# Both parts of the normalised input as one moving operand of 512 columns, in a hybrid MLA and RWKV-7 encoder block

## The chip, the cores and the metric

One core of one Trainium2 chip runs the whole block. The time is that of one execution in device microseconds; before the change the median of 3 runs was 874.93 us (874.09 to 885.55).

## What is computed

One encoder layer on 256 positions of width 2048, batch 1, all in float32. The reference, cut to its products:

```
h    = rms_norm(x, g_pre)                       # 256 x 2048
proj = h @ w_in                                 # 2048 x 10688: q_a, kv_a, k_rope | r, k, v, low-rank parts | z_mla, z_rwkv | gates
q, kv = rms_norm(q_a) @ wq_b, rms_norm(kv_a) @ wkv_b
y_mla  = softmax attention, 8 heads of 128 + 64 rotary, 256 keys
y_rwkv = bidirectional RWKV-7 recurrence, 16 heads of 64, with a group norm and a bonus
merged = sigmoid(gate_mla) * ((y_mla * silu(z_mla)) @ w_br_mla) + sigmoid(gate_rwkv) * ((y_rwkv * silu(z_rwkv)) @ w_br_rwkv)
x + rms_norm(merged @ w_out, g_post)
```

## The kernel before, in words

**Two parts.** Every large product is done in float32r, in two parts: a tensor v is hi (v rounded by a copy) and lo = v - hi, and a product is hi hi + hi lo + lo hi, three TensorE passes. The weights are split on the way. A chunk of up to 128 x 1024 weights is loaded into one of 3 *raw* buffers by the SP queue; ScalarE copies it to *whi* (L327), VectorE subtracts into *wlo* (L330), with 3 buffers of each.

**Transposed products.** A projection task (`in_task`, through `cm_task`) makes 256 output channels x 256 positions: two halves of 128 channels, 16 steps of 128 rows of the weights (k), and for each the three passes at L396 to L398. The weights are stationary (128 x 128), h is the moving operand of 256 columns: *hhi* and *hlo*, each 128 x 16 x 256. Both halves of a task fill one PSUM bank (128 x 512). There are 32 such tasks besides the 8 of the second gate (`gate_rwkv_task`): 12 for r, k and v (`rwkv_tasks`), 8 of the first gate (`gate_mla_task`), 8 for z (`z_task`), 4 low-rank ones of attention (`low_rank_task`). A first product of the low-rank parts (L1531 onwards, four tiles of 96, 96, 128 and 128 channels) opens the kernel. The branch products (`um_task`, `ur_task`) have the same three passes over 8 steps; the output projection (`out_task`, L1334 to L1336) has the activations stationary and weights of 512 columns moving.

**The end of a task** reads its bank. r, k and v go through `mix` (two scaled ScalarE copies out of PSUM at L422, a VectorE addition, two VectorE operations); z through a tanh and one VectorE operation; the gates through a tanh; the low-rank ones through one copy (L549).

**Banks.** Of 8 PSUM banks, 3 (`DB`, in the trace d) serve the tasks and 5 (`MB`, m) the recurrence, the group sums, the transposes and attention; the key-value tasks move one from `MB` to `DB`, and the output projection takes all.

**The recurrence.** Four quads of 4 heads each. A quad is prepared (decay, keys, values), then `chunks_of` forms the masked products (L797), inverts triangular blocks of 32 x 32 on VectorE and goes through 4 steps: short passes (L912 to L944), between which one ScalarE and one VectorE copy bring 64 x 256 out of PSUM. A group norm follows. A quad's products wait for the quad before.

**The order.** The instructions of all engines are put in order by a planner at build time (`Streams`). Each part is a stream (a generator) that asks for an engine with a cost; the planner keeps the time at which each engine is free, adds a lag to each hand-over, and takes the request that can start first, by rank. `Free` holds lists of buffers or banks: `take` waits until one is in the list, `give` puts it back. A stream runs ahead of the time it asks for, so a buffer is back in the list as soon as its giver has been planned. The projection (`mm_stream`) has the lowest rank and fills TensorE. All engines then work through their lists in this order.

The sequence of tasks: the low-rank parts, r, k and v of the first quad, first gate, z and low-rank tasks mixed with the next quads' r, k and v, then `GPRE` second-gate tasks, 4 key-value tasks (they wait for the last quad), 4 query tasks with `MIX` second-gate tasks between, the 8 attention-branch tasks, the 8 recurrent-branch tasks, 4 output tasks. The tanh of a second-gate task is kept in a place that has come free: in the recurrence's buffers *u8* or *uv*, or in one of the general buffers (`W`) where more than `KEEP2` are free.

Of the kernel before, what the change touches and what calls it, by code (L numbers as in the profile page):

```python
# [15 lines left out]
S = 256  # L16
D = 2048
# [11 lines left out]
GPRE, MIX = 4, [0, 1, 1, 1]  # L29
# [9 lines left out]
KEEP, KEEP2 = 6, 9  # L39
# [4 lines left out]
class Streams:  # L44
# [6 lines left out]
    def __init__(self):  # L51
        self.free = dict.fromkeys("PADGS", 0.0)
        self.live = []
        self.used = dict.fromkeys("PADGS", 0.0)
        self.table = None
        self.mode = "128x128"

    def add(self, gen, rank, t=0.0):
        s = [gen, rank, t, None]
# [18 lines left out]
    def run(self, until=None):  # L78
        while self.live and not (until and until()):
            moved = True  # L80
            while moved:
                moved = False
                for s in list(self.live):
                    while s in self.live and s[3][0] in "WT" and (s[3][0] == "T" or s[3][1]()):
                        if s[3][0] == "T":
                            s[2] = max(s[2], s[3][1])
                        self._next(s, s[2])
                        moved = True
            if until and until():
# [19 lines left out]
            e, cost = s[3][0], s[3][1]  # L109
            if e == "P":  # L110
# [13 lines left out]
class Free:  # L124


    def __init__(self, tiles):
        self.tiles = list(tiles)
# [26 lines left out]
def encoder_block_kernel(  # L155
# [52 lines left out]
    hhi, hlo = sb([128, KT, S], "hhi", dt=F32R), sb([128, KT, S], "hlo", dt=F32R)  # L208
# [4 lines left out]
    W = Free(works[:-1])  # L213
    MB = Free(pps.tile([128, 512], F32, tag=f"m{i}", bufs=1, name=f"m{i}") for i in range(5))
    DB = Free(pps.tile([128, 512], F32, tag=f"d{i}", bufs=1, name=f"d{i}") for i in range(3))
# [7 lines left out]
    QP = Free(qpads)  # L223
# [15 lines left out]

    O = Streams()  # L240
# [130 lines left out]
    def cm_task(src, nk, xhi, xlo, mt, wd, end, kc=4, load_fn=None, ready=None, kready=None, k_first=0,  # L371
                begin=None, pairs=None, first_alone=False):

        parts = []
        nb = (len(mt) + 1) // 2
# [3 lines left out]
        for i, k0 in enumerate(k0s):  # L379
# [23 lines left out]
        def take():  # L403
            b = []
            for _ in range(nb):
                b.append((yield from DB.take()))
            return b

        add_task(parts, begin or take, end, ready)
# [56 lines left out]
    def ev_second(b):  # L466
        yield ("W", lambda: len(have.get("part", ())) == 2)
        for p, m, t, B in zip(b, (96, 128), have["part"], (DB, MB)):
            yield ("D", cD(512))
            tt(w2d(t)[0:m], w2d(t)[0:m], p2(p)[0:m], ALU.add)  # L470
            B.give(p)
# [48 lines left out]
    def ev_z(b, o):  # L520

        z = p2(b[0])
# [15 lines left out]
    def gate_mla_task(g):  # L538
        def end(b):
            yield ("A", cA(512), None, "exp")  # L540
            act.activation(m16[:, 2 * g:2 * g + 2], p2(b[0]), AF.Tanh, scale=0.5)
            DB.give(*b)
        in_task(GM0 + 256 * g, end)

    def low_rank_task(c0, key):
        def end(b):
            t = yield from W.take(KEEP)
            yield ("A", cA(512))
            act.copy(w2d(t), p2(b[0]))  # L549
            DB.give(*b)  # L550
# [492 lines left out]
    def wkv_task(g):  # L1043
        wkv_v = wkv_b.rearrange("(k p) c -> p k c", p=128)

        def begin():
            if g == 0:
                yield ("W", lambda: quads[3].done and len(MB.tiles) > 1)
                DB.give(MB.tiles.pop())
# [12 lines left out]
            a = yield from DB.take()  # L1062
# [591 lines left out]
```

## Time and profile before

| | |
|---|---|
| runs | 874.93 us median (874.09 to 885.55) |
| the profiled execution | 872.72 us, its span 870.9 us |
| TensorE busy, passes | 848.3 us (97%), 8112 |
| TensorE weight loads busy | 810.0 us (93%) |
| VectorE busy | 659.3 us (76%) |
| ScalarE busy | 501.1 us (58%) |
| granted TensorE clock | 0.998 |

In the rows, PE is TensorE, PEld its weight loads, DVE VectorE, ACT ScalarE, SP the queue that issues the loads. A name such as d<-hhi,whi is output <- moving operand, stationary operand; L396 is line 396 of the kernel before. Passes are pipelined: a pass's record lasts about 0.28 us although the next begins 0.12 us after it, so short waits do not show as idle time.

### The profile page before, as it was taken

The numbers are of one execution on the slowest core, as the hardware profiler recorded it, in microseconds if no ns is written. First come the engines' busy times: TensorE is split into PE (matmuls) and PEld (weight loads), VectorE is DVE, ScalarE is ACT, GpSimd is POOL, SyncE is SP. The second block draws the span as 40 slices with busy tenths as digits, with TensorE's granted clock in tenths as the row PEclk, the third lists the DMA queues.
The fourth block names the chain that finished last, engine by engine and source line by source line (L and its number), as shares of the span: only waits on it lengthen the run. The fifth ranks groups of instructions, "written<-read, shape, count | busy, mean of one in ns | idle before, by whom it ended". The sixth has DMA issues, their size and how long they took to land.

```text
span 870.9 us, 19398 instructions
## 1 busy us (share of the span) xinstructions
PE 848.3 (97%) x8112; PEld 810.0 (93%) x8112; DVE 659.3 (76%) x1082; ACT 501.1 (58%) x797; POOL 30.7 (4%) x66
## 2 busy tenths in 40 slices
PE   9999999999999999999999999999999999999996
PEld 8999999988899998999889999899999999998884
DVE  5878898868987878988789878775867556775554
ACT  6777644487544578354776445586766434444442
POOL 4110000000000000000000000000000000000000
PEclk9999999999999999999999999999999999999999
DMA  9565646633376523565423665346444675555553
GB/s 286 169 181 148 176 129 187 169 99 90 101 212 177 161 68 97 158 193 169 132 76 96 195 188 152 98 149 186 136 128 147 232 257 190 176 193 193 194 195 119
DMA packets 123528, 139.41 MB, mean 160 GB/s; under 512 B 6704, under 2 KB 110512, under 8 KB 123056
## 3 DMA queue, kind: packets, MB, share of 16 engines
q1 hardware_dynamic: 121664, 135.16, 52.4%
q0 software_dynamic: 768, 1.57, 0.6%
q10 hardware_dynamic: 1008, 1.44, 0.5%
q8 instruction: 63, 1.03, 0.5%
q14 instruction: 25, 0.20, 0.1%
HBM read 136.05 MB, written 2.10 MB: 159 GB/s over the span
## 4 chain that ended last, share of the span: by engine, by line
PE 73%; DVE 14%; ACT 8%; issue 2%; DMA 2%; DVEq 0%; ACTq 0%
PE d L396 16%; PE d L398 16%; PE d L397 15%; DVE wlo L330 4%; PE m L1334 2%; PE m L1335 2%; PE m L1336 2%; ACT whi L327 2%; DVE work L191 2%; PE m L398 2%; PE m L396 2%; PE m L397 2%; PE d L1335 1%; PE d L1334 1%; PE d L1336 1%
## 5 line engine op out<-in xcount | busy, mean ns | idle before, releaser
L327 ACT CAST whi<-raw 128x1024 fp32r<-128x1024 f32 (+3 forms) x252 | 252.8, 1004 | 254.2 <-PE d L397 155.1
L330 DVE TENSOR_TENSOR wlo<-raw,whi 128x1024 fp32r<-128x1024 f32 (+3 forms) x250 | 292.4, 1171 | 125.0 <-ACT whi L327 123.4
L396 PE MATMUL d<-hhi,whi 128*128 128x256 f32 (+1 forms) x1296 | 375.1, 289 | 0.0
L398 PE MATMUL d<-hhi,wlo 128*128 128x256 f32 (+1 forms) x1296 | 366.5, 283 | 2.3 <-DVE wlo L330 2.3
L397 PE MATMUL d<-hlo,whi 128*128 128x256 f32 (+1 forms) x1296 | 366.2, 283 | 0.0
L396 PEld LDWEIGHTS d<-hhi,whi 128*128 128x128 f32 (+1 forms) x1296 | 246.8, 190 | 4.5
L398 PEld LDWEIGHTS d<-hhi,wlo 128*128 128x128 f32 (+1 forms) x1296 | 246.9, 190 | 2.7 <-DVE wlo L330 2.7
L397 PEld LDWEIGHTS d<-hlo,whi 128*128 128x128 f32 (+1 forms) x1296 | 247.1, 191 | 0.1
L191 DVE TENSOR_TENSOR work<-work,work 128x512 f32<-128x512 f32 (+5 forms) x64 | 38.8, 612 | 3.9 <-ACT work L575 1.2
L191 DVE TENSOR_TENSOR u<-u,tmp 128x30 f32<-128x30 f32 (+7 forms) x120 | 29.9, 250 | 3.0
L191 DVE TENSOR_TENSOR tmp<-u 128x30 f32<-128x30 f32 (+7 forms) x120 | 29.8, 249 | 2.9
L396 PE MATMUL d<-b,whi 128*128 128x256 f32 x96 | 27.1, 282 | 0.0
L398 PE MATMUL d<-b,wlo 128*128 128x256 f32 x96 | 27.1, 282 | 0.0
L398 PE MATMUL d<-ar,wlo 128*128 128x256 f32 x96 | 27.0, 281 | 0.0
L397 PE MATMUL d<-work,whi 128*128 128x256 f32 x96 | 26.9, 280 | 0.0
L397 PE MATMUL d<-ar,whi 128*128 128x256 f32 x96 | 26.9, 280 | 0.0
L396 PE MATMUL d<-ar,whi 128*128 128x256 f32 x96 | 26.8, 279 | 0.0
L1334 PE MATMUL m<-whi,hhi 128*128 128x512 f32 x60 | 23.3, 389 | 0.0
L1335 PE MATMUL m<-wlo,hhi 128*128 128x512 f32 x60 | 23.3, 389 | 0.0
L1336 PE MATMUL m<-whi,hlo 128*128 128x512 f32 x60 | 23.3, 389 | 0.0
L191 DVE TENSOR_TENSOR g<-m,mask 128x512 f32<-128x512 f32 x32 | 20.6, 686 | 0.0
L797 PE MATMUL m<-ar,u 64*128 64x128 f32 x256 | 19.2, 285 | 0.3 <-DVE g L191 0.3
(334 smaller groups left out, 1487.3 us busy)
## 6 DMA issues: line engine op xcount, KB each, us to landing
raw<-in_w_in_dram SPq DMA_DIRECT2D x160, 512.0 KB, 3.9
raw<-in_w_out_dram SPq DMA_DIRECT2D x32, 512.0 KB, 3.6
raw<-in_w_br_mla_dram SPq DMA_DIRECT2D x16, 512.0 KB, 4.0
raw<-in_w_br_rwkv_dram SPq DMA_DIRECT2D x16, 512.0 KB, 3.3
raw<-in_mla_wkv_b_dram SPq DMA_DIRECT2D x8, 512.0 KB, 3.9
raw<-in_mla_wq_b_dram SPq DMA_DIRECT2D x8, 384.0 KB, 3.3
raw<-in_w_in_dram SPq DMA_DIRECT2D x7, 384.0 KB, 5.3
g<-in_x_dram SPq DMA_DIRECT2D x2, 1024.0 KB, 6.9
```

The source lines that it names most:

```text
L191: dve.tensor_tensor(out=o, in0=a, in1=b, op=op)
L327: act.copy(dst(c.hi), src(raw))
L330: eng.tensor_tensor(out=dst(c.lo), in0=src(raw), in1=dst(c.hi).bitcast(F32), op=ALU.subtract)
L396: pe.matmul(o, hi[:, c:c + m], xhi(k), start=k == k_first and i % 2 == 0, stop=False)
L397: pe.matmul(o, hi[:, c:c + m], xlo(k), start=False, stop=False)
L398: pe.matmul(o, lo[:, c:c + m], xhi(k), start=False, stop=last)
L797: pe.matmul(m[:, q * 128:q * 128 + 128], z.kb[R64[h], d, j, q], z.ar[d][R64[h], j, q], start=q == 0, stop=q == 3)
L1334: pe.matmul(banks[t], hhi[:, k, T], hi, start=k == 0, stop=False)
L1335: pe.matmul(banks[t], hhi[:, k, T], lo, start=False, stop=False)
L1336: pe.matmul(banks[t], hlo[:, k, T], hi, start=False, stop=k == KT - 1)
```

## The change

Everything below is one change.

- *hhi* and *hlo* become the two halves of one tensor *hh* (128 x 2 x 16 x 256). For the 32 projection tasks named above, the two passes with the high part of the weights become one of 512 columns (both parts of h, in two pieces); the pass with the low part stays at 256 columns. The second gate keeps the three passes (`both=None`), and so does the first low-rank product.
- Each half of such a task now has a bank of its own: the first 256 columns hold hi hi + lo hi, the other 256 hi lo. The new `total` copies the second half of each bank to SBUF (ScalarE) and adds the first half (VectorE); the ends of the tasks go on from SBUF.
- The banks are 4 and 4; a task takes two.
- In the planner, a buffer has the time at which its giver's last operation ended, and a stream that takes it can't start before; a stream that waited for a condition goes on from the time at which it was met; the next request of a stream on the same engine has no lag.
- The recurrent-branch tasks come before the attention-branch tasks, so the sum of both, its halving and its split are made at the end of `um_task`; the split of the recurrence's output waits for the key-value tasks alone. The attention output's high part goes to *uv* instead of *ar*, so second-gate results go to *u8* or general buffers.
- `GPRE`, `MIX` and `KEEP2` are 6, [0, 1, 1, 0] and 5.

The diff, cut to its core:

```
-GPRE, MIX = 4, [0, 1, 1, 1]
+GPRE, MIX = 6, [0, 1, 1, 0]
...
-KEEP, KEEP2 = 6, 9
+KEEP, KEEP2 = 6, 5
...
     def _next(self, s, value):
+        self.now = s[2]
...
-                    while s in self.live and s[3][0] in "WT" and (s[3][0] == "T" or s[3][1]()):
-                        if s[3][0] == "T":
+                    while s in self.live and s[3][0] in "WTF" and (s[3][0] != "W" or s[3][1]()):
+                        if s[3][0] == "W":
+
+                            s[2] = max(s[2], self.now if len(s[3]) > 2 else 0.0)
+                        else:
                             s[2] = max(s[2], s[3][1])
+                        if s[3][0] == "F":
+                            s[5] = max(s[5], s[3][1])
                         self._next(s, s[2])
                         moved = True
+            for s in self.live:
+                if s[3][0] == "W" and len(s[3]) == 2:
+                    s[3] = (*s[3], True)
...
+                    if s[4] == q[0] and ready == s[2]:
+
+                        ready -= self.LAG[q[0]]
+                    ready = max(ready, s[5])
...
     def take(self, keep=0):
         yield ("W", lambda: len(self.tiles) > keep)
-        return self.tiles.pop(0)
+        t = self.tiles.pop(0)
+        yield ("F", self.since.get(id(t), 0.0))
+        return t
 
     def give(self, *tiles):
-        self.tiles.extend(tiles)
+        for t in tiles:
+            self.tiles.append(t)
+            self.since[id(t)] = self.order.now
...
-    hhi, hlo = sb([128, KT, S], "hhi", dt=F32R), sb([128, KT, S], "hlo", dt=F32R)
+
+    hh = sb([128, 2, KT, S], "hh", dt=F32R)
+    hhi, hlo = hh[:, 0], hh[:, 1]
...
-    MB = Free(pps.tile([128, 512], F32, tag=f"m{i}", bufs=1, name=f"m{i}") for i in range(5))
-    DB = Free(pps.tile([128, 512], F32, tag=f"d{i}", bufs=1, name=f"d{i}") for i in range(3))
+    O = Streams()
+    W = Free(O, works[:-1])
+    MB = Free(O, (pps.tile([128, 512], F32, tag=f"m{i}", bufs=1, name=f"m{i}") for i in range(4)))
+    DB = Free(O, (pps.tile([128, 512], F32, tag=f"d{i}", bufs=1, name=f"d{i}") for i in range(4)))
+
+    def take_banks(n):
+        b = []
+        for _ in range(n):
+            b.append((yield from DB.take()))
+        return b
...
+                        if both:
+
+                            o = p2(banks[i])[0:m]
+                            pe.matmul(o, hi[:, c:c + m], both(k), start=k == k_first, stop=False)
+                            pe.matmul(o[:, 0], lo[:, c:c + m], xhi(k), start=False, stop=k == nk - 1)
+                            continue
                         o = p2(banks[i // 2])[0:m, i % 2]
                         last = k == nk - 1 and (i % 2 == 1 or i == len(mt) - 1)
                         pe.matmul(o, hi[:, c:c + m], xhi(k), start=k == k_first and i % 2 == 0, stop=False)
                         pe.matmul(o, hi[:, c:c + m], xlo(k), start=False, stop=False)
                         pe.matmul(o, lo[:, c:c + m], xhi(k), start=False, stop=last)
 
-                steps.append((len(mt) * 3 * 0.119, mm) + (((lambda k=k: kready(k)),) if kready else ()))
+                steps.append((len(mt) * (0.347 if both else 3 * 0.119), mm) + (((lambda k=k: kready(k)),) if kready else ()))
...
+        kw.setdefault("both", lambda k: hh[:, :, k])
         cm_task(w_in_v[:, :, c0:c0 + w], KT, *HX, mt, w, end, **kw)
+
+    def total(b, o):
+
+        for i in range(2):
+            yield ("A", cA(256) - 0.05)
+            act.copy(o[:, i], p2(b[i])[:, 1])
+        for i in range(2):
+            yield ("D", cD(256))
+            tt(o[:, i], p2(b[i])[:, 0], o[:, i], ALU.add)
+            DB.give(b[i])
...
-                yield from mix(p2(b[0]), 128, V_MU + 8 * n + 2 * Q, w2d(t))
-                DB.give(*b)
+                yield from total(b, w2d(t))
+                yield from mix(w2d(t), 128, V_MU + 8 * n + 2 * Q, w2d(t))
...
+        yield from total(b, o)
         t = yield from W.take()
         yield ("A", cA(512), None, "exp")
-        act.activation(w2d(t), z, AF.Tanh, scale=0.5)
+        act.activation(w2d(t), o, AF.Tanh, scale=0.5)
         yield ("D", cD(512))
-        stt(o, w2d(t), 1.0, z, ALU.add, ALU.mult)
+        stt(o, w2d(t), 1.0, o, ALU.add, ALU.mult)
         W.give(t)
-        DB.give(*b)
...
+            o = m16[:, 2 * g:2 * g + 2]
+            yield from total(b, o)
             yield ("A", cA(512), None, "exp")
-            act.activation(m16[:, 2 * g:2 * g + 2], p2(b[0]), AF.Tanh, scale=0.5)
-            DB.give(*b)
+            act.activation(o, o, AF.Tanh, scale=0.5)
...
-            yield ("A", cA(512))
-            act.copy(w2d(t), p2(b[0]))
-            DB.give(*b)
+            yield from total(b, w2d(t))
...
+            hi = att["ymh", g] = sb([128, 2, 256], "uv", 4, F32R)
...
-            have["um"] = g
-
-        branch_task(w_br_mla, g, lambda k: att["ymh"][:, k], lambda k: att["yml", k // 2][:, k % 2], end,
+            yield ("D", cD(512))
+            tt(o, o, th2[g], ALU.add)
+            G2 = slice(2 * g, 2 * g + 2)
+            yield from half_split(o, hh[:, 0, G2], hh[:, 1, G2], 512)
+            have["merged"] = g
+            have["merged_t"] = O.free["D"]
...
-            return [n for n, free in (("u8", room["u8"] and quads[3].u8_free), ("uv", room["uv"] and quads[3].done),
-                                      ("work", len(W.tiles) > KEEP2)) if free]
+            return [n for n, free in (("u8", room["u8"] and quads[3].u8_free), ("work", len(W.tiles) > KEEP2)) if free]
...
-        in_task(GR0 + 256 * g, end)
+        in_task(GR0 + 256 * g, end, both=None)
...
-        yield ("W", lambda: "ymh" in att and all((n, g) in have for n in ("kv", "q") for g in range(4)))
+        yield ("W", lambda: all(("kv", g) in have for g in range(4)))
...
+        ur_task(g)
+    for g in range(8):
         um_task(g)
-    for g in range(8):
-        ur_task(g)
```

## Rows read from the trace of the kernel before

**Rows 1.** The page: span, busy time, share, instructions of each engine.

```profile
span 870.9 us, 19398 instructions
PE 848.3 (97%) x8112; PEld 810.0 (93%) x8112; DVE 659.3 (76%) x1082; ACT 501.1 (58%) x797; POOL 30.7 (4%) x66
```

**Rows 2.** Timeline of PE, input projection (start, length): passes 1 and 38.

```profile
251.74 0.28 PE L396 MATMUL d<-hhi,whi 128*128 128x256 f32 x1
...
256.18 0.28 PE L397 MATMUL d<-hlo,whi 128*128 128x256 f32 x1
```

**Rows 3.** Timeline of PE, output projection: passes 1 and 29.

```profile
799.78 0.39 PE L1334 MATMUL m<-whi,hhi 128*128 128x512 f32 x1
...
806.13 0.39 PE L1335 MATMUL d<-wlo,hhi 128*128 128x512 f32 x1
```

**Rows 4.** Windows: length, busy (count) PE, PEld, DVE, ACT, POOL; clock; DMA.

```profile
175.00:240.00 65.00, 61.61 (x813) 56.57 (x812) 54.53 (x83) 47.46 (x86) 4.17 (x9) 1.00 0.35 97
240.00:296.00 56.00, 56.00 (x528) 55.69 (x526) 47.54 (x94) 25.62 (x30) 0.12 (x1) 1.00 0.67 188
296.00:350.00 54.00, 51.56 (x728) 46.83 (x728) 43.69 (x71) 41.68 (x78) 3.16 (x7) 1.00 0.36 97
410.00:480.00 70.00, 66.31 (x917) 61.66 (x915) 59.99 (x86) 49.87 (x87) 3.21 (x8) 1.00 0.37 102
530.00:575.00 45.00, 44.03 (x712) 41.02 (x711) 33.83 (x57) 29.09 (x53) 0.61 (x2) 1.00 0.41 118
575.00:680.00 105.00, 104.61 (x851) 102.77 (x851) 76.22 (x156) 70.27 (x142) 0.00 (x0) 1.00 0.55 161
```

**Rows 5.** Waits of PE: who <- for whom: us, times, longest.

```profile
PE m L923 <- DVE work L918: 3.1, 8, 0.7
PE d L398 <- DVE wlo L330: 2.3, 2, 1.2
PE m L587 <- ACT work L435: 1.3, 2, 0.7
```

**Rows 6.** Groups of PE by shape: high weights on hhi; count | busy, mean.

```profile
L396 PE MATMUL d<-hhi,whi 128*128 128x256 f32 x1264 | 365.8, 289 | 0.0
...
L396 PE MATMUL m<-hhi,whi 128*128 128x256 f32 x48 | 13.7, 286 | 0.0
```

**Rows 7.** Timeline of PE, key-value product: passes 1 and 49.

```profile
589.90 0.28 PE L1086 MATMUL d<-whi,b 128*128 128x256 f32 x1
...
595.58 0.28 PE L1086 MATMUL d<-whi,b 128*128 128x256 f32 x1
```

**Rows 8.** Groups of ACT and DVE by shape: count | busy, mean | idle.

```profile
L1205 ACT COPY work<-m 128x256 f32<-128x256 f32 x16 | 5.8, 377 | 1.8 <-PE m L1203 1.8
L549 ACT COPY work<-d 128x512 f32<-128x512 f32 x4 | 2.3, 578 | 0.0
L541 ACT ACTIVATE m<-d 128x512 f32<-128x512 f32 x8 | 4.7, 588 | 0.0
L573 ACT ACTIVATE work<-work 128x512 f32<-128x512 f32 x8 | 5.0, 631 | 0.1
...
L330 DVE TENSOR_TENSOR wlo<-raw,whi 128x1024 fp32r<-128x1024 f32 x227 | 277.5, 1224 | 114.4 <-ACT whi L327 112.7
L191 DVE TENSOR_TENSOR work<-m,work 128x256 f32<-128x256 f32 x8 | 3.4, 422 | 3.9 <-PE m L1212 3.9
```

**Rows 9.** The same, ACT: copies that empty a recurrence step's bank.

```profile
L884 ACT COPY work<-m 128x128 f32<-128x128 f32 x16 | 4.2, 264 | 0.1
L882 ACT COPY yr<-m 128x128 f32<-128x128 f32 x16 | 4.2, 260 | 7.2 <-PE m L944 7.1
```

**Rows 10.** Timeline: first pass, last pass, end of the stores.

```profile
1.07 0.58 PE L1414 MATMUL m<-ones 128*128 128x128 f32 x1 [1.07 <-POOL ones L250]
...
862.51 0.40 PE L1336 MATMUL m<-uv,hlo 128*128 128x512 f32 x1
...
865.31 2.46 ACTq L1386 DMA_DIRECT2D out_dram<-m  x3
```

More of the change, by code (lines that the diff above doesn't have):

```diff
@@ L56, in __init__ @@
         self.mode = "128x128"
+        self.now = 0.0
     def add(self, gen, rank, t=0.0):
-        s = [gen, rank, t, None]
+        s = [gen, rank, t, None, "", 0.0]
         self.live.append(s)
@@ L124, with __init__ @@
 class Free:
-    def __init__(self, tiles):
-        self.tiles = list(tiles)
+    def __init__(self, order, tiles):
+        self.order, self.tiles, self.since = order, list(tiles), {}
     def take(self, keep=0):
         yield ("W", lambda: len(self.tiles) > keep)
-        return self.tiles.pop(0)
+        t = self.tiles.pop(0)
+        yield ("F", self.since.get(id(t), 0.0))
+        return t
     def give(self, *tiles):
-        self.tiles.extend(tiles)
+        for t in tiles:
+            self.tiles.append(t)
+            self.since[id(t)] = self.order.now
 def cA(n, aps=0):
@@ L371, in cm_task @@
     def cm_task(src, nk, xhi, xlo, mt, wd, end, kc=4, load_fn=None, ready=None, kready=None, k_first=0,
[L372 removed]
+                pairs=None, first_alone=False, both=None):
         parts = []
[L375 removed]
         k0s = list(range(k_first, nk, kc))
@@ L398, in mm @@
                         pe.matmul(o, lo[:, c:c + m], xhi(k), start=False, stop=last)
-                steps.append((len(mt) * 3 * 0.119, mm) + (((lambda k=k: kready(k)),) if kready else ()))
+                steps.append((len(mt) * (0.347 if both else 3 * 0.119), mm) + (((lambda k=k: kready(k)),) if kready else ()))
             parts.append((load, list(pairs(k0, kc)) if pairs else plain(kc * wd), steps))
[L403 to L409, printed above, removed]
+        add_task(parts, lambda: take_banks(len(mt) if both else (len(mt) + 1) // 2), end, ready)
     HX = (lambda k: hhi[:, k]), (lambda k: hlo[:, k])
@@ L467, in ev_second @@
         yield ("W", lambda: len(have.get("part", ())) == 2)
-        for p, m, t, B in zip(b, (96, 128), have["part"], (DB, MB)):
+        for p, m, t in zip(b, (96, 128), have["part"]):
             yield ("D", cD(512))
             tt(w2d(t)[0:m], w2d(t)[0:m], p2(p)[0:m], ALU.add)
-            B.give(p)
+            DB.give(p)
         yield from ev_wd(have["part"][0])
@@ L1047, in begin @@
             if g == 0:
-                yield ("W", lambda: quads[3].done and len(MB.tiles) > 1)
-                DB.give(MB.tiles.pop())
+                yield ("W", lambda: quads[3].done)
                 att["kT"] = sb([128, 2, 8, 256], "g16", dt=F32R)
@@ L1061, in begin @@
                     tt(t[R64[i]], kr[R64[i]], att["kr"][0][R64[i]].bitcast(F32), ALU.subtract)
-            a = yield from DB.take()
-            b = yield from DB.take()
-            return a, b
+            return (yield from take_banks(2))
         parts = []
@@ L1104, in wq_task @@
         wq_v = wq_b.rearrange("(k p) (h c) -> p k h c", p=128, c=192)
-        def begin():
-            a = yield from DB.take()
-            b = yield from DB.take()
-            return a, b
         parts = []
@@ L1156, in end @@
                 O.add(head(g, i), 1, O.free["D"])
-        add_task(parts, begin, end, lambda: have["qhl"][1] if "qhl" in have else None)
+        add_task(parts, lambda: take_banks(2), end, lambda: have["qhl"][1] if "qhl" in have else None)
     def half_split(src, hi, lo, n):
@@ L1299, in end @@
             DB.give(*b)
-            yield ("D", cD(512))
-            tt(o, o, m16[:, G2], ALU.add)
-            yield from half_split(o, hhi[:, G2], hlo[:, G2], 512)
-            have["merged"] = g
-            have["merged_t"] = O.free["D"]
         branch_task(w_br_rwkv, g, lambda k: have["yr"][0][:, k], lambda k: have["yr"][1][:, k], end,
@@ L1319, in begin @@
                 MB.tiles.clear()
-            a = yield from DB.take()
-            b = yield from DB.take()
-            return a, b
+            return (yield from take_banks(2))
         parts, more = [], []
@@ L1362, in end @@
                 yield from gain(b, t)
+                DB.give(b[t])
             fin["left"] -= 2
@@ L1523, in pairs_first @@
                ("kr", 0 if k0 < 2 else 2 if k0 < 8 else 8))
-    def begin_second():
-        a = yield from DB.take()
-        b = yield from MB.take()
-        return a, b
     LORA = [(0, 96), (128, 96), (256, 128), (384, 128)]
```

26 lines of the change are left out of this document (9 added, 17 removed).

## The prediction

> **What bounds the kernel now.** I read the busy times first. TensorE is busy for 848.3 of the 870.9 us of the span, VectorE for 659.3, ScalarE for 501.1 [rows 1]: what is saved on TensorE shortens the run, as long as the other two still deliver in time. A busy matmul is not yet a full TensorE, so I read start against start next. In an undisturbed stretch of input projection, 37 steps take from 251.74 to 256.18 us, 0.1200 us for each pass of 256 columns [rows 2]. In the output projection 28 steps of 512 columns take 6.35 us, 0.2268 us each [rows 3]. Twice the columns cost 1.89 times as much. At the granted clock of 1.00 [rows 4], the 2.4 GHz level, 256 columns stream in 106.7 ns and 512 in 213.3, so about 13.3 ns of each pass is a fixed part, at both lengths.
>
> Then the stretches. Four of them hold the step-by-step part of a quad: 175 to 240, 296 to 350, 410 to 480 and 530 to 575 us. There TensorE shows 3.4, 2.4, 3.7 and 1.0 us without work, 10.5 us together, while between and after them it shows none or 0.4 [rows 4]. The list of TensorE's waits names what it lacks: results of VectorE and ScalarE inside the recurrence and the group sums, and now and then a low part of the weights [rows 5]. No transfer stands among them. In the same stretches VectorE is busy for 54.5 of 65, 43.7 of 54 and 60.0 of 70 us [rows 4]: it is the engine with the least room.
>
> **What the change does to each.**
>
> *The passes.* Of 1264 + 48 = 1312 full-width passes on the high part of h [rows 6], the 8 second-gate tasks keep the old form (8 x 32 = 256) and so do the two full-width tiles of the low-rank product (32). That leaves 1024 triples of 256 + 256 + 256 columns that become pairs of 512 + 256: 32 tasks with 16 steps and two halves. The weight loads fall by 1024 too and stay hidden behind passes. By these spacings [rows 2, 3] a triple takes 360 ns and a pair 227 + 120 = 347: 13.2 ns less, 13.5 us in all. The new operand lies in two pieces, far apart, which no pass of 512 columns does now. The nearest row is the key-value product, where one of three passes that feed the value half streams two pieces of 128 columns: 48 steps take 5.68 us, 0.1183 each, pieces and whole ones alike [rows 7]. So I add nothing for it. That stretch also gives the lower bound, 2 x 118.3 - 226.8 = 9.8 ns or 10.0 us. The projection is nearer to its own spacing [rows 2], but whether its 120 comes down to 118 plus a half or stays is open; I take 12 us, between 10.0 and 13.5.
>
> The Trainium skill (TensorE: Matmul & The Clock Gate, the section on 56 ns against 53.3 ns) puts the fixed part of a warm pass at about 2.5 ns. By that the merging would be worth 1024 x 2.5 = 2.6 us; the rows of both lengths show five times as much, and they decide.
>
> *Bringing the two halves together.* Each of the 32 tasks now leaves two banks, and *total* needs two ScalarE copies of 256 columns out of PSUM and two VectorE additions. The nearest copies take 0.377 us, the nearest additions (one operand in PSUM) 0.422 [rows 8]. ScalarE: 32 x 0.754 = 24.1 us more, less four copies of 0.578 in the low-rank tasks = 2.3, plus 16 x 0.043 since the tanh now reads SBUF (0.631 against 0.588) = 0.7; 22.5 us net. VectorE: 32 x 0.844 = 27.0 us more. What covers it: TensorE's 11.1 us per task. On average the cover holds: even if as many tasks as fit ended in the 70 us stretch (6.3), VectorE would go from 60.0 to 65.3. I cost it at nothing. If the cover is gone, each microsecond that VectorE lacks in a stretch is one that TensorE waits. Behind an addition that waits for its copy stands the next subtraction for the low part of the weights (1.224 us [rows 8]), for which TensorE waits, and so does the next load on the SP queue, which reuses its buffer; three such buffers give about two chunks, 5.5 us, of slack.
>
> *Banks.* Tasks get 4 banks, two each, so a task's banks must come free within the next task's 11.1 us; the evacuation takes 1.6 us if nothing is in its way: nothing lost. The recurrence and attention have 4 instead of 5. No row shows one lacking. A missing bank can't bring a gain; the dearest case is that each of the 16 steps (4 quads of 4) waits until the two copies of 0.26 us that empty the oldest bank are done [rows 9]: 16 x 0.52 = 8.4 us. I take 0, because TensorE has projection passes to do meanwhile; 8.4 stays for the range.
>
> *The order.* A buffer counts as free only when its giver's last operation has ended, a stream that waited goes on from the time of its waking, and a stream's next operation on the same engine follows without the hand-over's lag. All engines run in order, so a right forecast shows as fewer waits of TensorE. Bounds: all visible idle time outside the head and tail is worth 870.9 - 848.3 - 1.1 - 8.0 = 13.5 us (the lead-in and the tail [rows 10]); on the other side, if each hand-over came later by one addition, 4 quads x (4 steps x 3 + 4 group sums) = 64 hand-overs x 0.422 = 27 us. VectorE's extra load and the truer times pull against each other. I take a gain of 3 us, nearer to the small waits of the list [rows 5] than to either end.
>
> *What is moved.* The eight recurrent-branch products now run before the eight attention-branch ones, as fill while the heads finish, and two more second-gate tasks before the key-value product. Their passes, splits and loads (16 + 16 chunks on SP) are the same in number. In 575 to 680 us TensorE lacks only 0.4 us [rows 4], so there is next to nothing to win. The last step before the output projection has the same four operations as before, and the tail after the last pass, 862.9 to 870.9 us [rows 10], is not touched.
>
> *Sum* against the profiled execution's own 872.72 us (870.9 and 1.8 around it): 872.7 - 12 - 3 = 857.7. The median of the runs shown, 874.93, is 2.2 us and the lowest, 874.09, 1.4 us above that execution; with 1.5 for it I forecast 859 us.
>
> **Rivals.**
>
> *The order wins most of the waits (25%).* For it: 10.5 us of waits stand exactly where the planner's picture of buffers and hand-overs matters. Against: they are waits for data, and VectorE gets fuller. 10 instead of 3 us: about 852 us (847 to 856).
>
> *The fifth bank is missed (20%).* For it: a step of the recurrence holds a bank for its outputs while two more are filled. Against: no wait of that kind now. It gives back 8.4: 868 us (864 to 873).
>
> *The merging pays almost nothing (4%).* Either a pass over two far pieces starts twice, as two passes of 256 columns do, or the fixed part goes with the columns when it is h that moves: the pair takes 360 ns, 0 is saved, and the time is 872.7 - 3 + 1.5 = 871 us with the order's gain, 874 without. The measured spacings speak against it [rows 2, 3, 7].
>
> The 2.5 ns of the Trainium skill's clock-gate section would lead to nearly this time by another way: 2.6 us saved, about 869 to 871 us. The 13.3 ns at both lengths leave that little.
>
> *Slower: the additions delay the recurrence (6%).* VectorE runs in order, and in 410 to 480 us it has 10 us free of 70. If the pairs of additions stand ahead of the small copies between the recurrence's passes, TensorE, also in order, waits behind each. The full 64 hand-overs x 0.422 give +27 against -12: 889 us. It is slower than before from 12 / 0.422 = 28 late hand-overs on. For it: VectorE's share there; against: TensorE has projection passes to do between the hand-overs, and the planner counts the additions. Only if more than one addition stands in the way does it pass 892; I give that half of this case.
>
> **How the numbers follow.** Forecast as above 45%, with a range of its own from 854 to 864. About 2% (17.5 us) is what a measurement of this kernel tells from no change: the bounds are 857.4 and 892.4 us. Faster by over 2%: the first rival's 25% and some 12 of the forecast's 45, which lie below 857.4: 37%. Slower by over 2%: 3%. The rest, 60%. For 8 in 10 I leave out the lowest part of the first rival and everything above the missing bank: 848 to 872 us.
>
> **What would show it.** Right: pairs start 0.227 + 0.120 us apart; TensorE has 1024 fewer passes; VectorE is busy for about 686 and ScalarE for about 524 us; idle time in the four stretches is no more than 10.5 us together. Wrong: a 512-column pass on h that takes 0.24 us; waits of the low parts or of the recurrence's copies on additions of *total*; waits of the recurrence for a bank's evacuation; a pause before the key-value product.

## The result, and the profile after

The changed kernel takes 884.70 us (median of 20 runs, 882.65 to 886.69) against 874.15 us (20 runs) for the kernel before beside it: ratio 1.0125, 95% interval 1.0118 to 1.0131. It is 1.25% **slower**, by some 11 us. 859 us was forecast, and 848 to 872 us was the range; the result lies above both. Below, a run's time is compared by its ratio to the kernel before measured beside it, turned into microseconds at 874.15 (0.001 is 0.87 us).

The page of the changed kernel (its profiled execution took 886.17 us, 13.5 more than the one before, where the medians differ by 10.6): span, busy times and the two groups of the merged passes (busy, mean ns, idle before):

```profile
span 884.4 us, 17506 instructions
...
PE 847.7 (96%) x7088; PEld 758.0 (86%) x7088; DVE 682.0 (77%) x1146; ACT 519.4 (59%) x857; POOL 31.0 (4%) x66
...
L422 PE MATMUL d<-hh,whi 128*128 128x512 f32 x1024 | 368.7, 401 | 0.0
L423 PE MATMUL d<-hh,wlo 128*128 128x256 f32 x1024 | 288.6, 282 | 5.0 <-DVE wlo L356 5.0
```

Against [rows 1] TensorE has 1024 passes fewer, but is busy for 847.7 us, only 0.6 less, and idle for 36.7 us instead of 22.6. Is the pass itself slower than thought? The timeline of TensorE in an undisturbed stretch of projection says no:

```profile
251.88 0.39 PE L422 MATMUL d<-hh,whi 128*128 128x512 f32 x1
252.11 0.28 PE L423 MATMUL d<-hh,wlo 128*128 128x256 f32 x1
...
255.70 0.39 PE L422 MATMUL d<-hh,whi 128*128 128x512 f32 x1
```

Eleven pairs take 3.82 us, 0.3473 each, where a triple took 0.3600 [rows 2]: 12.7 ns less, or 13.0 us over 1024 pairs. Those 13.0 us are saved; by the medians some 24 are lost elsewhere, by the two profiled executions 26.5. The windows of [rows 4], and then four short ones (length; busy PE, PEld, DVE, ACT, POOL; granted clock; DMA):

```profile
175.00:240.00 65.00, 61.82 (x772) 51.34 (x772) 51.49 (x84) 47.27 (x90) 3.23 (x8) 0.97 0.38 109
240.00:296.00 56.00, 53.16 (x307) 46.65 (x306) 53.04 (x104) 29.11 (x39) 0.00 (x0) 1.00 0.60 169
296.00:350.00 54.00, 50.74 (x683) 42.51 (x682) 42.89 (x69) 41.39 (x80) 3.27 (x8) 1.00 0.38 104
410.00:480.00 70.00, 63.48 (x764) 53.29 (x763) 59.67 (x92) 49.88 (x90) 3.29 (x8) 0.98 0.44 125
530.00:575.00 45.00, 42.93 (x691) 40.00 (x691) 35.85 (x59) 26.18 (x45) 0.61 (x2) 1.00 0.45 127
575.00:680.00 105.00, 102.76 (x842) 101.27 (x842) 69.71 (x120) 66.78 (x120) 0.00 (x0) 0.98 0.55 161
```

```profile
187.25:190.65 3.40, 3.40 (x28) 2.81 (x30) 1.12 (x3) 1.53 (x3) 0.12 (x1) 0.50 0.50 150
371.60:374.95 3.35, 3.35 (x12) 2.87 (x11) 3.25 (x6) 2.44 (x4) 0.00 (x0) 0.50 0.97 291
477.40:484.20 6.80, 4.79 (x26) 4.03 (x26) 6.18 (x12) 5.32 (x11) 0.00 (x0) 0.50 0.28 77
651.50:654.85 3.35, 3.35 (x18) 3.35 (x18) 3.11 (x11) 1.90 (x7) 0.00 (x0) 0.50 0.64 166
```

The four recurrence stretches now show 15.0 us without work on TensorE instead of 10.5, the projection between the first two 2.8 instead of none, and the last window 2.2 instead of 0.4. And there are four stretches, 16.9 us together, in which the granted clock is 0.50, the 1.2 GHz level, and TensorE is busy for 14.9 us; at 2.4 GHz half of that, some 7.4 us, would do. Before, every window of [rows 4] stands at 1.00.

So the ledger of the span: idle +14.1 us; busy 12.4 us above what the saved passes leave (848.3 - 13.0 = 835.3), of which the lower clock is 7.4. About 5 us of the busy time I can't place: stalls shorter than a pass's record may hide in it, which isn't shown. 14.1 + 12.4 - 13.0 = 13.5, the difference of the spans.

TensorE's longest waits (who, for whom: us, times, longest), the answer to [rows 5], where the longest was 1.2:

```profile
PE m L831 <- DVE g L210: 5.5, 2, 5.0
PE m L957 <- DVE work L952: 5.2, 6, 1.6
PE d L423 <- DVE wlo L356: 5.0, 3, 2.8
...
PE m L1229 <- DVE work L216: 1.6, 1, 1.6
```

The longest, 5.04 us, ends at 479.41. The timeline around it, from the last pass of the 28th merged task on:

```profile
451.09 0.28 PE L423 MATMUL d<-hh,wlo 128*128 128x256 f32 x1
...
472.18 0.40 PE L422 MATMUL d<-hh,whi 128*128 128x512 f32 x1
...
472.41 0.28 PE L423 MATMUL d<-hh,wlo 128*128 128x256 f32 x1
472.44 1.22 DVE L356 TENSOR_TENSOR wlo<-raw,whi 128x1024 fp32r<-128x1024 f32 x1
...
473.71 0.66 PE L839 MATMUL m<-iv,u 128*128 128x128 f32 x4
...
477.52 0.65 ACT L447 COPY work<-d 128x256 f32<-128x256 f32 x2
...
479.41 2.41 PE L831 MATMUL m<-ar,u 64*128 64x128 f32 x16 [5.04 <-DVE g L210]
...
479.87 0.74 DVE L210 TENSOR_TENSOR work<-d,work 128x256 f32<-128x256 f32 x2
...
482.51 0.78 PE L422 MATMUL d<-hh,whi 128*128 128x512 f32 x1
...
483.38 0.66 ACT L447 COPY work<-d 128x256 f32<-128x256 f32 x2
```

The pass at 472.18 is the 928th of its kind, 29 x 32: the first 29 merged tasks are done, and none is begun. A chunk of weights lies ready from 473.66 on. But the next pass of any task comes 10.3 us later, after *total* has emptied the first two of the four banks: its copies run at 477.52 and its additions from 479.87 to 480.61.

Whose banks are these? Tasks are emptied in the order in which they end, so the copies at 477.52 belong to the 28th task and those at 483.38 to the 29th. The 28th's last pass starts at 451.09: its banks are held for 29 us after it, where the prediction had 1.6. The copies did not stand in a queue all that time; ScalarE runs 37 other operations in those 26 us:

```profile
451.37:477.52 26.15, 22.40 (x272) 18.67 (x272) 21.29 (x33) 20.06 (x37) 2.15 (x5) 1.00 0.36 102
```

The reason stands in the source, and the words on the end of a task above leave it out: the end of an r, k, v, z or low-rank task takes a general buffer first, and only where more than `KEEP` = 6 are free. The 28th task is a z task and the 29th a low-rank one. Followed through the planner, the end of the 28th waits for that buffer from its last pass on, and *total* is put in order only when it has it. No run changed the general buffers, so what this request costs by itself is not measured.

The profile names a hand-over of the recurrence (g), since that is what TensorE's next instruction waited for; what is missing is a pass of a task to do meanwhile. That it is missing for want of a bank is read from this order of events; the experiments test it.

A long hold is not new. In the kernel before, the bank of a low-rank task is held for 22 us, but there the other two banks were two more tasks:

```profile
439.22 0.28 PE L398 MATMUL d<-hhi,wlo 128*128 128x256 f32 x1
...
460.80 0.57 ACT L549 COPY work<-d 128x512 f32<-128x512 f32 x1
```

The groups of *total* have the sizes forecast:

```profile
L447 ACT COPY work<-d 128x256 f32<-128x256 f32 x48 | 15.6, 370 | 8.0 <-PE d L423 7.9
...
L210 DVE TENSOR_TENSOR work<-d,work 128x256 f32<-128x256 f32 x48 | 18.7, 417 | 3.7 <-ACT work L447 3.6
```

0.370 and 0.417 us, where [rows 8] gave 0.377 and 0.422. ScalarE waits 7.9 us at these copies for a task's last pass: a copy at the head of its list holds up what stands behind it. What that costs is not shown.

### The profile page after: what moved, and what is told of

Its sections match the earlier page's. It is cut to its first block, busy times and chain, and to the rows that moved or that the text cites. A ratio compares the mean times of both kernels' runs of the same rounds, so it can differ in the third digit from the quotient of the medians.

```text
span 884.4 us, 17506 instructions
## 1 busy us (share of the span) xinstructions
PE 847.7 (96%) x7088; PEld 758.0 (86%) x7088; DVE 682.0 (77%) x1146; ACT 519.4 (59%) x857; POOL 31.0 (4%) x66
## 3 DMA queue, kind: packets, MB, share of 16 engines
q0 software_dynamic: 768, 1.57, 0.6%
## 4 chain that ended last, share of the span: by engine, by line
PE 66%; DVE 17%; ACT 10%; issue 3%; DMA 3%; SPq 0%; DVEq 0%; ACTq 0%
PE d L422 16%; PE d L423 8%; PE d L427 7%; PE d L429 7%; PE d L428 7%; DVE wlo L356 5%; DVE work L210 2%; ACT whi L353 2%; DMA raw<-in_w_in_dram 2%; PE m L1352 2%; PE m L1354 2%; PE m L1353 2%; PE d L1353 2%; PE d L1352 2%; PE d L1354 2%
## 5 line engine op out<-in xcount | busy, mean ns | idle before, releaser
L422 PE MATMUL d<-hh,whi 128*128 128x512 f32 x1024 | 368.7, 401 | 0.0
L423 PE MATMUL d<-hh,wlo 128*128 128x256 f32 x1024 | 288.6, 282 | 5.0 <-DVE wlo L356 5.0
L422 PEld LDWEIGHTS d<-hh,whi 128*128 128x128 f32 x1024 | 193.4, 189 | 43.6
L423 PEld LDWEIGHTS d<-hh,wlo 128*128 128x128 f32 x1024 | 194.7, 190 | 6.4 <-DVE wlo L356 6.3
L427 PE MATMUL d<-hh,whi 128*128 128x256 f32 (+1 forms) x320 | 93.2, 291 | 0.2 <-ACT hh L1471 0.2
L428 PE MATMUL d<-hh,whi 128*128 128x256 f32 (+1 forms) x320 | 90.7, 284 | 0.7 <-DVE hh L213 0.7
L429 PE MATMUL d<-hh,wlo 128*128 128x256 f32 (+1 forms) x320 | 90.7, 283 | 0.0
L427 PEld LDWEIGHTS d<-hh,whi 128*128 128x128 f32 (+1 forms) x320 | 60.7, 190 | 1.3 <-ACT hh L1471 0.4
L428 PEld LDWEIGHTS d<-hh,whi 128*128 128x128 f32 (+1 forms) x320 | 60.8, 190 | 0.9 <-DVE hh L213 0.9
L429 PEld LDWEIGHTS d<-hh,wlo 128*128 128x128 f32 (+1 forms) x320 | 60.6, 189 | 0.0
L429 PE MATMUL d<-uv,wlo 128*128 128x256 f32 x128 | 36.0, 281 | 0.0
L427 PE MATMUL d<-uv,whi 128*128 128x256 f32 x128 | 35.8, 280 | 0.0
```

What stands on the lines that cost most here:

```text
L422: pe.matmul(o, hi[:, c:c + m], both(k), start=k == k_first, stop=False)
L423: pe.matmul(o[:, 0], lo[:, c:c + m], xhi(k), start=False, stop=k == nk - 1)
L427: pe.matmul(o, hi[:, c:c + m], xhi(k), start=k == k_first and i % 2 == 0, stop=False)
L428: pe.matmul(o, hi[:, c:c + m], xlo(k), start=False, stop=False)
L429: pe.matmul(o, lo[:, c:c + m], xhi(k), start=False, stop=last)
```

## Experiments: the planner and the places

**The planner's rules of before, with everything else of the change.**

```diff
-                            s[2] = max(s[2], self.now if len(s[3]) > 2 else 0.0)
+                            pass
-                    if s[4] == q[0] and ready == s[2]:
-                        ready -= self.LAG[q[0]]
-        yield ("F", self.since.get(id(t), 0.0))
+        yield ("F", 0.0)
```

> The changed kernel with the planner of before: no time at which a buffer comes free, a stream that waited is not set to its time of waking, and the lag stays between a stream's operations on one engine. Everything else of the change stays (merged pass, additions, 4 and 4 banks, sequence of tasks). Theory A (the new planner's order leaves TensorE waiting): 860 to 868 us, near the forecast, clock 0.996 or more, visible waits of TensorE 12 us or less. Theory B (the additions fill VectorE and delay the recurrence whatever the order): 880 us or more, clock still under 0.992. Theory C (4 instead of 5 banks): as B, 878 or more.

Measured 896.67 us, 1.027 (1.0254 to 1.0287). The new rules are not at fault: without them the change costs 12.7 us more.

**The new planner alone**, in the kernel before, with its banks and passes.

> The kernel before with the new planner alone: three passes of 256 columns, 3 and 5 banks, no additions, old sequence of tasks. Theory A: slower than before by 8 to 25 us, 882 to 899 us, with longer waits and stretches at the lower clock. Theory B and C: no loss, 866 to 876 us.

872.76 us, 0.9997 (0.9988 to 1.0007). There the better picture of buffers is worth nothing that can be measured; in the changed kernel it is worth those 12.7 us.

**All of the change but merging and *total***: one bank a task, 4 banks for the recurrence and 4 for tasks, the new sequence and places. Then the same with 5 and 3 banks.

```diff
-        kw.setdefault("both", lambda k: hh[:, :, k])
...
-                yield from total(b, w2d(t))
-                yield from mix(w2d(t), 128, V_MU + 8 * n + 2 * Q, w2d(t))
+                yield from mix(p2(b[0]), 128, V_MU + 8 * n + 2 * Q, w2d(t))
+                DB.give(*b)
```

> The changed kernel (new planner, new sequence of tasks, 4 and 4 banks) with the merging taken back whole: three passes of 256, one bank for a task, the ends of before, no copies and additions of total. Theory B (the extra VectorE and ScalarE work delays the recurrence): 868 to 876 us, clock 0.995 or more. Theory C (the recurrence lacks its fifth bank): 880 us or more. Theory D (the new sequence and the places of the second gate cost the time): 880 or more here too, and in the next run as well.

> The same with the banks of before, 5 for the recurrence and 3 for the tasks, one handed over at the key-value tasks. Theory B: as the run with 4 and 4, within 3 us. Theory C: 8 us or more below it. Theory D: as slow as it, 880 or more.

874.78 us, 1.002 (1.001 to 1.003), and 874.58, 1.0018 (1.0009 to 1.0028). The fifth recurrence bank is not missed, and the moved tasks cost 1.7 us at most: the rest of the loss sits in merging, its banks and *total*. In the run with 4 and 4 banks a z task's bank is held for 29 us too (last pass at 427.56, last read at 456.93), while TensorE is busy for 30.66 of the 31 us, since other banks are free:

```profile
427.56 0.28 PE L429 MATMUL d<-hh,wlo 128*128 128x256 f32 x1
...
455.03 0.60 ACT L560 ACTIVATE work<-d 128x512 f32<-128x512 f32 x1
...
456.93 0.68 DVE L213 SCALAR_TENSOR_TENSOR work<-work,d 128x512 f32<-128x512 f32 x1
```

```profile
427.00:458.00 31.00, 30.66 (x296) 29.53 (x297) 23.55 (x34) 24.31 (x41) 1.16 (x3) 1.00 0.35 103
```

**The planner counts more for *total***, in case its low costs made a bad order:

```diff
-            yield ("A", cA(256) - 0.05)
+            yield ("A", cA(256) + 0.05)
-            yield ("D", cD(256))
+            yield ("D", cD(256) + 0.03)
```

> The changed kernel; in the planner alone each copy of total costs 0.36 instead of 0.26 us and each addition 0.38 instead of 0.35, near to what the trace shows. Same instructions, another order. If the waits come from the planner's too low costs of total: 872 to 879 us. Theory B as a matter of load: within 4 us of 884.7.

887.34 us, 1.0161 (1.0142 to 1.0179): slower still, so not that. The instructions are the same; their order alone moves the time by 3.1 us, and that much must be allowed for where other runs below have an order of their own.

## Experiments: merging, two banks, *total*

**Merging undone in place**: the order of after, each pass of 512 as two of 256.

```diff
-                            pe.matmul(o, hi[:, c:c + m], both(k), start=k == k_first, stop=False)
+                            pe.matmul(o[:, 0], hi[:, c:c + m], xhi(k), start=k == k_first, stop=False)
+                            pe.matmul(o[:, 1], hi[:, c:c + m], xlo(k), start=False, stop=False)
```

> The changed kernel in its own order, each pass of 512 columns on h issued as two passes of 256 into the two halves of the same bank: the merging alone undone. If the merging is worth its 10 to 12 us in place: 893 to 898 us. If the waits swallow it (TensorE would only wait longer where it is faster): 885 to 889 us.

887.11 us, 1.016 (1.0143 to 1.0176). Of the 13.0 us of TensorE's time that the merged passes save, the run gets 3.1 in this order: the rest falls into waits.

**The additions left out**, in the order of after (the `tt` line of *total* deleted; the planner still counts it and gives the banks back at the same place). The result lacks the first halves.

> The changed kernel in its own order, with the 64 additions left out (the planner still counts them, so all engines keep their lists but for these): the first half of each bank is not added, so that part of the projection is missing. Theory B: the 27 us of VectorE are what delays, 862 to 870 us, clock back over 0.995. Theory A: most waits stay, 876 to 885 us. C: 880 to 885.

877.93 us, 1.0056 (1.0038 to 1.0074): the 64 additions cost 6.0 us. The longest wait is not among them. It stays as long, 5.05 us, so VectorE's additions don't make it:

```profile
472.76 1.65 PE L830 MATMUL m<-ar,u 64*128 64x128 f32 x10 [5.05 <-DVE g L210]
```

**Merged passes and two banks, without *total***; then the same with each 512 pass as two of 256, the planner told so. In both the ends read the first bank alone, so the other bank and the second halves are missing from the result.

> The run without merging (4 and 4 banks, ends of before), now with the merged passes and two banks for a task, but no copies and additions: the ends read the first bank alone, as before, so the other bank and the second halves are missing from the result. Theory B (copies and additions of total are what costs): the merging's 1024 x 12.7 ns = 13.0 us come in whole or nearly, 860 to 866 us, clock 0.995 or more. Theory E (the recurrence, not TensorE, sets the pace in its stretches, so passes saved there turn into waits anyway; or two banks a task are too few): 868 us or more.

> The run with merged passes and no total, with each pass of 512 columns issued as two of 256 into the two halves of the same bank and planned so: three passes a triple as before, two banks a task, the ends read the first bank alone (the rest is missing from the result). Theory F (two of four banks for each task leave TensorE only one task ahead of the evacuation): 878 us or more, with waits of passes for a bank that VectorE still reads. Theory E (passes saved in the recurrence's stretches turn into waits, the banks do not matter): 873 to 877 us, as the run without merging.

878.33 us, 1.0068 (1.0052 to 1.0085), and 884.65 us, 1.0125 (1.0109 to 1.014). In the second, without merging, *total* or an added operation, two banks a task bring the whole loss. TensorE's longest wait of each of the two:

```profile
PE d L422 <- DVE work L213: 12.0, 2, 10.1
```

```profile
PE d L422 <- DVE work L213: 8.2, 1, 8.2
```

The first pass of a task waits for the operation that reads the bank of an earlier task. Here it stands in the list by name.

**One bank a task, but only two tasks in flight**: the kernel with 4 + 4 banks of above, two of its task banks held back until the key-value product.

```diff
+    spare = [DB.tiles.pop() for _ in range(2)]
...
+                DB.give(*spare)
```

> The run without merging and with 4 and 4 banks, where only 2 of the tasks' 4 banks are given out until the key-value tasks: one bank a task, two tasks in flight as with the merging, passes and ends as before. Theory F: 879 us or more and long waits for a bank. Theory E: within 2 us of 874.8.

886.00 us, 1.0142 (1.0128 to 1.0156), 10.7 us more than with four. This is the same limit without merging, addition or second bank. In its timeline TensorE stops when 27 of the 32 tasks are done and the two banks hold a z and a low-rank task; the z task's last pass starts at 428.62, and its last read at 454.32, 26 us later:

```profile
428.62 0.28 PE L430 MATMUL d<-hh,wlo 128*128 128x256 f32 x1
...
446.64 0.28 PE L430 MATMUL d<-hh,wlo 128*128 128x256 f32 x1
...
454.32 0.68 DVE L213 SCALAR_TENSOR_TENSOR work<-work,d 128x512 f32<-128x512 f32 x1
...
455.06 0.58 PE L428 MATMUL d<-hh,whi 128*128 128x256 f32 x1 [8.14 <-DVE work L213]
...
455.44 0.42 PE L429 MATMUL d<-hh,whi 128*128 128x256 f32 x1
```

```profile
450.00:460.10 10.10, 5.04 (x29) 4.60 (x30) 7.84 (x14) 2.66 (x4) 0.00 (x0) 0.52 0.34 99
```

The wait of 8.14 us and the stretch at 1.2 GHz around its end (the window's row: 5.04 us busy at 0.52, about half of it lost) come to some 10.6 us, about the whole of the 10.7. So the loss by two tasks in flight is nearly all in one place: a z and a low-rank task hold both, and nothing is left to do. With four in flight the same hold costs TensorE nothing.

**Merging only the eight second-gate tasks**, with 4 + 4 banks, and with the banks of before (5 + 3) and the new planner.

```diff
-        in_task(GR0 + 256 * g, end, both=None)
+        in_task(GR0 + 256 * g, end, both=lambda k: hh[:, :, k])
```

> The run without merging and with 4 and 4 banks, but the 8 second-gate tasks merged (512 + 256, two banks, total). They run mostly after the recurrence, where VectorE has room. 8 x 32 pairs x 12 ns = 3.1 us. Theory B: 2 to 4 us below the run without merging. If merging gives nothing anywhere: within 1 us of it.

> The kernel before with the new planner and the merging in the 8 second-gate tasks alone, which run where VectorE has room; 3 and 5 banks, old sequence. 256 pairs x 12.7 ns = 3.3 us of TensorE. If its additions find room: 870 to 872 us, a little faster than before. If attention's hand-overs suffer: 873 us or more.

873.64 us, 1.0011 (1.0001 to 1.002): 0.8 us better than without, which is not clear of noise, of 3.3 by spacing (8 x 32 x 12.7 ns). And 878.82 us, 1.0061 (1.0049 to 1.0074): with three task banks it turns into a loss of 5.6 us. I had expected a gain there. Of three banks a merged task leaves one for the others; that this is the reason fits the two runs above and wasn't tried by itself.

## Experiments: VectorE's load, or when a bank comes free

**Fewer subtractions on VectorE**: every fourth weight chunk of a stretch has its low part made on GpSimd, in the changed kernel and in the kernel before with the new planner.

```diff
-                on, eng, cost = ("G", gp, 1.85) if i in WLG else ("D", dve, cD(n))
+                on, eng, cost = ("G", gp, 1.85) if i in WLG else ("G", gp, 2.65) if 20 <= i < 150 and i % 4 == 0 else ("D", dve, cD(n))
```

> The changed kernel with every fourth low part of the weights between chunks 20 and 150 (33 of them) subtracted on GpSimd instead of VectorE, planned at 2.65 us. It takes 33 x 1.2 = 40 us from VectorE, more than the additions brought. Theory B with VectorE as the late engine: 866 to 877 us. If ScalarE's copies or the order are what delays: 880 us or more.

> The kernel before with the new planner, and the same 33 low parts on GpSimd. If VectorE's load already holds TensorE up there: 864 to 870 us. If not: 871 to 875 us; if the two engines get in each other's way at the memory: 876 or more.

923.73 us, 1.058 (1.0552 to 1.0608), and 912.02 us, 1.0446 (1.0427 to 1.0466). Both lose 39 to 40 us, so it says nothing on what VectorE's load is worth; what the trace shows of it stands at the end.

**One copy and one addition of 512** per task, from two neighbouring banks held as one buffer:

```diff
+    dps = [pps.tile([128, 2, 512], F32, tag=f"d{i}", bufs=1, name=f"d{i}") for i in range(2)]
...
+        act.copy(o, p[:, :, 256:512])
+        tt(o, p[:, :, 0:256], o, ALU.add)
```

> The changed kernel with a task's two banks side by side, so that total is one ScalarE copy and one VectorE addition of 512 columns in two pieces, instead of two of 256 each. By the durations 0.59 against 0.75 and 0.69 against 0.84 us: 32 x 0.15 = 5 us less on each engine, and two instructions fewer in each hand-over. Theory B: 878 to 882 us. If load does not matter: 884 to 887.

902.76 us, 1.0344 (1.0328 to 1.0359). The experiment failed. Waits like this one appear, which I read as tasks with a single bank waiting for readers of the other, now that both are one buffer:

```profile
PE d L429 <- DVE m L213: 3.1, 4, 0.8
```

The changed kernel has none like it. The load can't be read from this run.

**Banks emptied by ScalarE alone**: four copies, both banks given back, then one addition of 512 from SBUF. The second halves take one more general buffer.

```diff
+            for h, to in ((0, o), (1, w2d(t))):
+                yield ("A", cA(256) + 0.05)
+                act.copy(to[:, i], p2(b[i])[:, h])
             DB.give(b[i])
+        yield ("D", cD(512))
+        tt(o, o, w2d(t), ALU.add)
```

> The changed kernel with ScalarE copying both halves of both banks out (four copies, 1.5 us a task, 24 us more of ScalarE in all), so that a bank is free without waiting for VectorE; one addition of 512 columns in SBUF follows. Theory F with VectorE as the holder: 872 to 881 us. If ScalarE's load matters as much: 885 us or more.

878.91 us, 1.0061 (1.0047 to 1.0074): 5.6 us faster than the change, though ScalarE is busier:

```profile
PE 842.5 (96%) x7088; PEld 752.5 (86%) x7088; DVE 679.6 (77%) x1114; ACT 536.2 (61%) x921; POOL 31.2 (4%) x66
```

ScalarE has 16.8 us more to do than in the change and VectorE only 2.4 less. That a bank no longer waits for its turn in VectorE's list fits the gain, but the order is another one too. The gain is about what the additions cost (6.0); what two banks cost is still there. One wait of 8.24 us for a bank is left, ending at 481.87, and that bank's last pass had started at 453.07: held for 29 us here too, whichever engine empties it. It still does not beat the kernel before, and no version here does beyond its uncertainty.

## Why the prediction was wrong

The **step that failed** is the one on banks: "a task's banks must come free within the next task's 11.1 us; the evacuation takes 1.6 us if nothing is in its way: nothing lost". It counted the four banks as room, and forgot what they were: before, three banks were three tasks in flight, and now four are two. And the evacuation does have something in its way: the end of a z or low-rank task first waits for a general buffer, and the 28th task's banks are held for 29 us instead of 1.6. The trace of the kernel before had a hold of 22 us already. The runs give the sum, each step with an uncertainty of 1.5 to 2 us from the runs, and with an order of its own:

- new planner, sequence and 4 + 4 banks: +1.7 us;
- two banks a task: +9.2 (10.7 when tasks in flight alone are halved);
- merged passes, replanned: -5.0, of 13.0 by spacing;
- *total*: +5.0; its additions alone, in the order of after, 6.0.

Together +10.9, as the change measures: each step is the difference of two runs in a row that leads from the kernel before to the change. The sizes hold for this row of steps; that two tasks in flight cost about the whole loss is shown twice, by the second step and by the run with one bank a task.

**The passes: right**, and sized well. 12 us was taken, 13.0 came, the two far pieces cost nothing, and no 512 pass takes 0.24 us. What was wrong is that they would all shorten the run. The prediction's opening, that what is saved on TensorE shortens the run "as long as the other two still deliver in time", holds the condition that failed. The Trainium skill's 2.5 ns of fixed cost for a warm pass (TensorE: Matmul & The Clock Gate, 56 ns against 53.3 ns) would save 2.6 us, close to the 3.1 of the split pass, but by another cause: the spacing of this trace is 12.7 ns shorter, five times as much.

***Total* costed at nothing: wrong by 5 to 6 us.** Its size was right (VectorE 682.0 us against 686 forecast, ScalarE 519.4 against 524). The argument went by average room, 65.3 of 70 us. What an addition costs where it stands in VectorE's list was left out. The run in which ScalarE empties the banks points to the place rather than the room, but does not single it out. The sign named for it, waits for the low parts of the weights, is there (5.0 us instead of 2.3), but it is as large with the additions left out (5.0), so they don't make it.

**The order: 3 us of gain, none came** alone (0.9997); within the change it is worth 12.7. That it hides part of the shortage that the change brings is my reading.

**What is moved: right** within 1.7 us, taken at nothing; nor does the tail change: the last pass starts at 876.01 us, 8.4 before the end, as before [rows 10].

**The rivals.** The fifth bank missed (20%): refuted by the pair with 4 + 4 and 5 + 3 banks; I looked for the shortage on the wrong side, among the recurrence's banks. Merging pays almost nothing (4%): 3.1 us in place, but not by the pass. Slower through additions (6%, 889 us): nearest in time and right in that the additions cost something, but its mechanism is half of the loss at most; its late hand-overs of one addition each would not appear with two tasks in flight and no addition at all, and 886.00 us does.

A rule of the Trainium skill (Perfetto Trace Analysis, the section on matmuls in Optimizing Tensor Performance) names both sides in one breath: independent groups of matmuls should rotate through PSUM banks so that the emptying of one overlaps the next, and larger matmuls are more efficient. These runs agree with both, and here they speak against each other: the larger matmul took a bank of rotation, and the rotation was worth more, 9.2 us against the 5.0 that arrived of 13.0.

**Open** are the 5 us of TensorE's busy time without a place, whether merging would pay its 13.0 us with more banks, and what an earlier general buffer for the ends of z and low-rank tasks would give back; no run tried the last two.

## What to carry to other kernels

Count buffers in tasks in flight, not in buffers: an edit that makes one task hold two of them halves the work that an in-order engine can fall back on while others are late. Time how long a buffer is held in the busiest stretch, from its last writer to its last reader in the trace, not by the durations of the operations that empty it; make sure that both belong to the same task, and look for what the reader itself has to be given first, here a buffer in SBUF. And before a saving on the bounding engine is counted, try the resource that it takes by itself: two tasks in flight without any of the gain showed the whole loss.

## What the runs showed of the hardware

**The clock falls after short waits, but not after each.** The stretches at 1.2 GHz in the changed kernel follow waits of 1.56 us (ending at 186.46), 1.83 (370.06) and 1.57 (650.34) after 0.8 to 1.5 us, and one begins inside the wait of 5.04. But the wait of 2.84 us that ends at 246.80 has none behind it: that window stands at 1.00. Nor has the wait of 1.57 us that ends at 639.97 in the run with 4 and 4 banks and no merging. A wait of TensorE can thus cost more than its length: three waits of 1.6 to 1.8 us stand ahead of 3.4 us each at half the clock, worth up to 1.7 more.

**GpSimd and VectorE get in each other's way.** A subtraction of 1024 columns takes 2.569 us on GpSimd, and some of VectorE's operations on two SBUF operands grow, while the group below with one in PSUM doesn't. From the changed kernel with the low parts on GpSimd, groups by shape:

```profile
L356 POOL TENSOR_TENSOR wlo<-raw,whi 128x1024 fp32r<-128x1024 f32 x33 | 84.8, 2569 | 423.9 <-ACT whi L353 400.8 <-PE d L422 12.6 <-PE d L423 10.5
```

```profile
L210 DVE TENSOR_TENSOR g<-m,mask 128x512 f32<-128x512 f32 x32 | 20.5, 681 | 3.2 <-PE m L831 3.2
...
L210 DVE TENSOR_TENSOR ar<-work,work 128x512 f32<-128x512 f32 x16 | 14.6, 934 | 0.1
```

Both took 686 ns in the kernel before; the one with an operand in PSUM (g<-m) stays at 681. The Trainium skill (SBUF — State Buffer, SBUF: two separate sides) says that VectorE with two SBUF inputs and GpSimd take a shared port pair by turns, each for a whole instruction; these rows agree: 934 against 681 ns. How much of the 39 to 40 us this makes, and how much GpSimd's longer subtraction, is not shown.
